# Two hybrid-mixer layers on one core: gates computed ahead by halves, one merge for all branches, another order in attention

## The chip, the cores and the metric

The kernel runs on one core of one Trainium2 chip. The metric is device time in microseconds of a whole execution, all weights and inputs in the chip's main memory at its start. Three executions of the kernel before were timed, and one more was profiled.

## The reference

Two layers of a hybrid mixer over 1024 latent tokens and 256 context tokens, model width 1024, in float32. In each layer the normalized and modulated input goes through one projection `w_in`, which feeds four branches of width 256: neighbourhood attention (A), latent attention (B), a bidirectional recurrent unit (C) and grouped-query attention (D). Each branch's result `y` is gated and merged:

```python
def merge_branches(ys, z, m, w_branch, w_out):
    zs = jnp.split(z, N_BRANCH, axis=-1)
    ms = jnp.split(m, N_BRANCH, axis=-1)
    acc = sum(jax.nn.sigmoid(ms[i]) * ((ys[i] * jax.nn.silu(zs[i])) @ w_branch[i]) for i in range(N_BRANCH))
    return acc @ w_out
# x <- LayerNorm(alpha * x + gate * merge_branches(...)) * ln_g + ln_b
```

The merge gates `m` are 4 x 1024 columns of the input projection, the largest part of it. In the first layer the context tokens take part in everything (1280 tokens, 10 tiles of 128); in the second the context has no output, so queries, gates and results are 1024 tokens (8 tiles). `shift`, `scale` and `gate` come from a small modulation product per layer.

## The kernel before, in words

Every float32 operand of a matmul is split in two parts, `hi` (ScalarE's cast to fp32r) and `lo` (VectorE's difference), and a product is three matmuls: hi x hi, hi x lo, lo x hi (`mm_a`, lines 276 to 278, tokens in rows; `mm_b`, lines 284 to 286, tokens in columns). `hi_lo` (lines 289, 290) splits activations, `split_w` (lines 238, 239) weights. The input of a layer is kept on the chip, split, as `xh` and `xl`.

A planner orders the instructions of each engine from the program text and gives tiles their buffers; a pool's tag has a fixed number of buffers, and an instruction that needs one waits until it is free. `wp` holds ten pairs of weight tiles (`whi`, `wlo`, 512 columns each) and two tiles for raw weights, `sl` 13 slots of 1280 columns for everything long (keys, values, probabilities, the sum, results), `tp` the short ones (`tmp` 3, `ph` 2, `pl` 2, `q` 3 buffers). `wide` is three banks of PSUM, taken in turn by `sbank`; `mm` has two more.

One layer runs: `g_proj` (projection of branch D), then `m_proj` and `a_proj` (B and A) woven with `lru` (C), then attention, then the merge, `last` and `outp`.

Attention works through twelve heads (four each of D, B, A), each in units of two or three query tiles; in the first layer a head begins with a short unit, the two context tiles with their 256 keys. For each query tile `scores` fills `wide` (line 639), VectorE copies it with the minimum (line 641), ScalarE takes the exponential (line 615). `values` then works through the blocks of 128 keys: `turn` transposes the probabilities (line 586) and splits them into `ph` and `pl`, `product` multiplies with the values (lines 593, 594). It is queued, and `pump` lets steps of it run between the scores of the following unit; each product follows its transposes by one block:

```python
            for i, b in enumerate(blocks):
                nx = turn(*b)
                tick()
                if st:
                    product(i - 1, *st)
                st = nx
                yield
```

`tick` draws from a generator that fills TensorE's time: `gates` computes the merge gates of the last two branches in `M_ORDER` = (2, 3, 1, 0), all eight chunks of 128 columns each, and stores them to memory (`gate_d`). `fetch` loads the next unit's queries and `ahead_kv` the next head's keys and values, both from SP's queue (lines 651, 653; 660, 665); the gates' weights are loaded, and the gates stored, from ScalarE's queue.

The merge goes through the first three branches, chunk by chunk and, within a chunk, by groups of tokens (256, 512 and 512 in the first layer, 512 and 512 in the second). For branches 2 and 3 a group is 24 matmuls for the gate (into `mm`) and 6 for the branch's product (into `wide`); for branch 1 the gate is loaded and 6 matmuls are left. ScalarE takes the sigmoid (line 993), VectorE multiplies (line 999), and the sum `acc[c]` is added to (line 1000), on POOL where the gate was loaded. In the first layer `modulation` steps are woven in. `last` does branch 0 in the same way with its own loop, and splits each chunk of the finished sum into `xh` and `xl` while it goes. `outp` multiplies with `w_out` tile by tile, two halves of 512 columns, adds the residual and normalizes (lines 1062 to 1071, statistics at line 197); for the first layer it also forms the next layer's `xh` and `xl`.

Of the kernel before, what the change touches and what calls it, by code (L numbers as in the profile page):

```python
# [16 lines left out]
D = 1024  # L17
# [19 lines left out]
G_PRE = 2  # L37
W_A = 30
W_B = 26
UNITS = [(2, 3), (5, 3), (8, 2)]  # L40
NBIAS = (E_N + M_N) * 64
# [5 lines left out]
def hybrid_kernel(ctx: ExitStack, tc, a):  # L47
# [8 lines left out]
    sm = ctx.enter_context(tc.tile_pool(name="sm", bufs=6))  # L56
# [60 lines left out]
    def spare():  # L117

        turns[0] += 1
        tag = ("tmp", "ph", "tmp", "pl", "tmp", "ph", "pl")[turns[0] % 7]  # L120
        return tp.tile([128, 512], F32, tag=tag, name=nm("spare"), bufs=3 if tag == "tmp" else 2)
# [72 lines left out]
    def row_stats(src):  # L194
        st = sm.tile([128, 2, 6], F32, tag="bnst", name=nm("bnst"))
# [36 lines left out]
    def split_w(raw, shape):  # L232
# [3 lines left out]
        hi = wp.tile([128, 512], F32R, tag="whi", name=nm("whi"))  # L236
        lo = wp.tile([128, 512], F32R, tag="wlo", name=nm("wlo"))
# [7 lines left out]
    def load_w(src, shape):  # L245
# [8 lines left out]
        return split_w(raw, shape)  # L254
# [37 lines left out]
    def layer(l, xh, xl, need_ctx, gate, finish, side, side2, ahead=None):  # L292
# [24 lines left out]
        gate_d = {i: dram([KC, 128, NT], F32, f"gates{i}") for i in M_ORDER[4 - G_PRE:]}  # L317
        u_d = [dram([2, 128, NT], F32, f"u{i}") for i in range(4)]

        def put_t(dst, t, first, src, rows=128):  # L320
# [6 lines left out]
            hi = tp.tile([128, 4, 128], F32R, tag="ph", name=nm("th"), bufs=2)  # L327
# [8 lines left out]
        def put_v(dst, t, src3):  # L336

            n = src3.shape[1]
            vt = tp.tile([128, 4, 128], F32R, tag="ph", name=nm("vt"), bufs=2)
# [226 lines left out]
        def attend(h, unit, qs, y, rcp, scores, vt):  # L566
# [7 lines left out]
            queue.append([values(64 * (h % 2), y, qts, blocks, pts, vt), len(blocks) + 1])  # L574

        def values(o, y, qts, blocks, pts, vt):
# [5 lines left out]
            def turn(vb, q0, cols):  # L582
# [4 lines left out]
                ph = tp.tile([128, 512], F32R, tag="ph", name=nm("ph"), bufs=2)  # L587
# [128 lines left out]
        def m_steps():  # L716
            gm, mrope_c, mrope_s, wraws, wu = pre[0]
            wm = [split_w(r, [128, 416]) for r in wraws]
# [23 lines left out]
            def second(t, has_q, y, kr):  # L742
# [4 lines left out]
                ch = tp.tile([128, 512], F32R, tag="ph", name=nm("ch"), bufs=2)  # L747
# [138 lines left out]
        def attention(jobs):  # L886
# [68 lines left out]
        for _ in att:  # L955
            pass
# [276 lines left out]
```

## Time and profile before

| | us |
|---|---|
| median of 3 runs | 3145.56 |
| lowest, highest | 3131.25, 3148.48 |
| profiled execution, its time | 3149.83 |
| its span, first to last instruction | 3148.0 |
| merge and `last`, first layer | 1157 to 1634 |
| attention, first and second layer | 423 to 1157, 2100 to 2738 |
| merge and `last`, second layer | 2738 to 3046 |

The mean granted clock of TensorE over the span is 0.949 of full speed. In what is cited from the trace, a name such as `m_att__ph` is a tile `ph` made in stage `m_att`, an arrow points from what is read to what is written (out<-in), L290 is line 290 of the kernel, and a bracket or a last column says how long the engine was idle and what ended that. PE is TensorE's matmuls, PEld its weight loads, DVE VectorE, ACT ScalarE, POOL GpSimd, SPq and ACTq the queues in which SP and ScalarE issue transfers. A busy time of PE is not full use: matmuls overlap, and one that stands with 0.39 us follows another every 0.23 us.

### The profile page before, as it was taken

The numbers are of one execution on the slowest core, as the hardware profiler recorded it, in microseconds if no ns is written. First come the engines' busy times: TensorE is split into PE (matmuls) and PEld (weight loads), VectorE is DVE, ScalarE is ACT, GpSimd is POOL, SyncE is SP. The second block draws the span as 40 slices with busy tenths as digits, with TensorE's granted clock in tenths as the row PEclk, the third lists the DMA queues.
The fourth block names the chain that finished last, engine by engine and source line by source line (L and its number), as shares of the span: only waits on it lengthen the run. The fifth ranks groups of instructions, "written<-read, shape, count | busy, mean of one in ns | idle before, by whom it ended". The sixth has DMA issues, their size and how long they took to land.

```text
span 3148.0 us, 39813 instructions
## 1 busy us (share of the span) xinstructions
PE 2837.8 (90%) x14458; PEld 2292.2 (73%) x14458; DVE 1554.1 (49%) x3147; ACT 1270.7 (40%) x2698; POOL 235.2 (7%) x327
## 2 busy tenths in 40 slices
PE   7987979998988999999789897998999897999878
PEld 3766868787877787776457685877887786788657
DVE  5653365554545551222368644366654464523366
ACT  4353364544444451111233435265544454512230
POOL 1210000000000000000342110000000000000141
PEclk9998989998999999999799999998999998999999
DMA  7232422222323222322462323322332233212252
GB/s 256 86 106 88 118 66 65 83 89 67 92 85 97 92 94 65 71 60 90 157 173 78 119 75 115 112 83 72 89 94 75 84 102 96 78 47 64 89 159 77
DMA packets 308782, 299.83 MB, mean 95 GB/s; under 512 B 24553, under 2 KB 245993, under 8 KB 308585
## 3 DMA queue, kind: packets, MB, share of 16 engines
q1 hardware_dynamic: 177384, 202.49, 21.3%
q10 hardware_dynamic: 131200, 94.79, 9.8%
q8 instruction: 114, 1.87, 0.3%
q14 instruction: 84, 0.68, 0.1%
HBM read 217.11 MB, written 80.10 MB: 94 GB/s over the span
## 4 chain that ended last, share of the span: by engine, by line
PE 65%; DMA 15%; DVE 7%; ACT 4%; POOL 3%; issue 3%; SPq 2%; ACTq 1%; POOLq 0%; DVEq 0%
PE wide L639 5%; PE merge__mm L284 4%; PE merge__mm L285 4%; PE merge__mm L286 4%; PE wide L284 2%; PE wide L285 2%; PE wide L286 2%; PE m_att__t L586 2%; PE a_att__mm L284 2%; PE a_att__mm L285 2%; PE a_att__mm L286 2%; DMA g_att__q<-start__qkg 2%; PE g_att__t L586 2%; PE m_att__mm L286 2%; PE m_att__mm L284 2%
## 5 line engine op out<-in xcount | busy, mean ns | idle before, releaser
L284 PE MATMUL merge__mm<-xh,merge__whi 128*128 128x512 f32 (+1 forms) x640 | 240.5, 376 | 1.2 <-DVE a_att__tmp L439 1.2
L285 PE MATMUL merge__mm<-xl,merge__whi 128*128 128x512 f32 (+1 forms) x640 | 236.7, 370 | 0.0
L286 PE MATMUL merge__mm<-xh,merge__wlo 128*128 128x512 f32 (+1 forms) x640 | 236.6, 370 | 0.0
L290 DVE TENSOR_TENSOR m_att__pl<-m_att__t,m_att__ph 128x384 fp32r<-128x384 f32 (+1 forms) x248 | 121.5, 507 | 141.3 <-ACT m_att__ph L289 138.2
L289 ACT CAST m_att__ph<-m_att__t 128x384 fp32r<-128x384 f32 (+1 forms) x248 | 105.7, 441 | 148.1 <-PE m_att__t L586 101.0
L238 ACT CAST merge__whi<-merge__wraw 128x512 fp32r<-128x512 f32 (+1 forms) x112 | 59.3, 530 | 236.0 <-PE merge__mm L285 179.3
L284 PEld LDWEIGHTS merge__mm<-xh,merge__whi 128*128 128x128 f32 x640 | 121.1, 189 | 41.5 <-issue 16.5
L239 DVE TENSOR_TENSOR merge__wlo<-merge__wraw,merge__whi 128x512 fp32r<-128x512 f32 (+1 forms) x112 | 64.5, 576 | 166.2 <-ACT merge__whi L238 158.4
L290 DVE TENSOR_TENSOR g_att__pl<-g_att__t,g_att__ph 128x384 fp32r<-128x384 f32 (+1 forms) x228 | 112.8, 514 | 68.0 <-ACT g_att__ph L289 64.6
L999 DVE TENSOR_TENSOR merge__tmp<-wide,merge__tmp 128x512 f32<-128x512 f32 (+1 forms) x80 | 50.9, 637 | 176.2 <-PE wide L286 168.3
L639 PE MATMUL wide<-g_att__ks,g_att__q 128*128 128x512 f32 (+1 forms) x400 | 112.4, 380 | 26.6 <-DMA g_att__q<-start__qkg 14.0
L286 PEld LDWEIGHTS merge__mm<-xh,merge__wlo 128*128 128x128 f32 x640 | 121.3, 189 | 20.7
L289 ACT CAST g_att__ph<-g_att__t 128x384 fp32r<-128x384 f32 (+1 forms) x228 | 99.6, 446 | 89.5 <-PE g_att__t L586 80.4
L285 PEld LDWEIGHTS merge__mm<-xl,merge__whi 128*128 128x128 f32 x640 | 121.2, 189 | 19.1
L284 PE MATMUL wide<-merge__uh,merge__whi 128*128 128x512 f32 (+1 forms) x240 | 100.5, 419 | 36.9 <-DVE merge__tmp L999 26.4
L284 PE MATMUL a_att__mm<-xh,a_att__whi 128*128 128x512 f32 (+1 forms) x320 | 126.2, 395 | 0.3 <-DVE a_att__tmp L439 0.3
L993 ACT ACTIVATE merge__tmp<-merge__mm 128x512 f32<-128x512 f32 (+1 forms) x80 | 44.2, 553 | 199.6 <-PE merge__mm L286 198.4
L593 PE MATMUL m_att__pv<-m_att__ph,m_att__vs 128*128 128x384 f32 (+1 forms) x228 | 88.8, 389 | 37.3 <-ACT m_att__ph L289 37.2
L285 PE MATMUL a_att__mm<-xl,a_att__whi 128*128 128x512 f32 (+1 forms) x320 | 121.9, 381 | 0.0
L641 DVE TENSOR_SCALAR_CACHE_REDUCE m_att__p<-wide 128x1280 f32<-128x1280 f32 (+1 forms) x72 | 98.7, 1371 | 46.1 <-PE wide L639 43.1
L286 PE MATMUL a_att__mm<-xh,a_att__wlo 128*128 128x512 f32 (+1 forms) x320 | 121.1, 380 | 0.0
L639 PE MATMUL wide<-m_att__ks,m_att__q 128*128 128x512 f32 (+1 forms) x400 | 120.8, 372 | 0.4 <-DVE m_att__p L641 0.4
(415 smaller groups left out, 8060.7 us busy)
## 6 DMA issues: line engine op xcount, KB each, us to landing
merge__wraw<-in_w_in_dram SPq DMA_DIRECT2D x64, 256.0 KB
mod__wm<-in_w_mod_dram SPq DMA_DIRECT2D x48, 256.0 KB
g_proj__wm<-in_w_mod_dram SPq DMA_DIRECT2D x16, 512.0 KB
a_att__wraw<-in_w_in_dram ACTq DMA_DIRECT2D x32, 256.0 KB
last__wraw<-in_w_out_dram SPq DMA_DIRECT2D x32, 256.0 KB
g_att__wraw<-in_w_in_dram ACTq DMA_DIRECT2D x28, 256.0 KB
m_att__wraw<-in_w_in_dram ACTq DMA_DIRECT2D x28, 256.0 KB
merge__wraw<-in_w_branch_dram SPq DMA_DIRECT2D x48, 128.0 KB
```

The costliest lines, as they stand in the source:

```text
L238: act.copy(hi[:, :n], raw[:, :n])
L239: dve.tensor_sub(lo[:, :n], raw[:, :n], hi[:, :n])
L284: pe.matmul(ps, wh, xh, start=first and k == 0, stop=False)
L285: pe.matmul(ps, wh, xl, start=False, stop=False)
L286: pe.matmul(ps, wl, xh, start=False, stop=last and k == nk - 1)
L289: act.copy(hi, src)
L290: dve.tensor_sub(lo, src, hi)
L586: pe.transpose(tb[:, i * 128:(i + 1) * 128], pts[q0 + i][:, col:col + 128], ident)
L593: pe.matmul(pv[:, qr], vt[:, vb, :], ph, start=i == 0, stop=False)
L639: pe.matmul(wide[:, c0:c0 + w], qs[:, j, qi * 128:(qi + 1) * 128], k[:, c0:c0 + w], start=j == 0, stop=j == len(ks) - 1)
L641: dve.tensor_scalar(pt[:, :nk], wide[:, :nk], -scale, None, ALU.mult, ALU.min, accum_out=nb)
L999: dve.tensor_mul(sgm[:, :g[1]], pb[:, :g[1]], sgm[:, :g[1]])
```

## The change

Gates computed ahead: `gate_d` has a tile for each odd chunk of every branch instead of all chunks of two branches, and `gates` goes through these. The merge goes through all four branches with computed (even) and loaded (odd) chunks in turn; `last` keeps only the loads of `w_out` and the splitting of the sum, by groups of 256 tokens over all eight chunks, after the whole merge. The second layer's modulation gate, which ran within `last`, is woven into the merge. `outp` begins with a batch of four tiles, first halves before second halves. In attention `product` follows `turn` by `AHEAD` = 2 blocks, `ph` has three buffers, `ahead_kv` is called at a head's second unit instead of its first, and TensorE's instructions keep the order of the program text (`manual_schedule`). `wp` has six pairs instead of ten, `sl` 16 slots instead of 13, and a `far` weight pair lies in a slot. Buffers of small tiles (`sm`, `bnst`) and the scratch of POOL's transfers shrink to make room.

```diff
-G_PRE = 2
+AHEAD = 2
...
-    wp = ctx.enter_context(tc.tile_pool(name="wp", bufs=10))
-    sl = ctx.enter_context(tc.tile_pool(name="sl", bufs=13))
+    wp = ctx.enter_context(tc.tile_pool(name="wp", bufs=6))
+    sl = ctx.enter_context(tc.tile_pool(name="sl", bufs=16))
...
-    def split_w(raw, shape):
+    def split_w(raw, shape, far=False):
...
-        hi = wp.tile([128, 512], F32R, tag="whi", name=nm("whi"))
-        lo = wp.tile([128, 512], F32R, tag="wlo", name=nm("wlo"))
+        if far:
+            both = slot(F32R, w=1024, s="wboth")
+            hi, lo = both[:, :512], both[:, 512:]
+        else:
+            hi = wp.tile([128, 512], F32R, tag="whi", name=nm("whi"))
+            lo = wp.tile([128, 512], F32R, tag="wlo", name=nm("wlo"))
...
-        return [load_w(w2[k * 128:(k + 1) * 128, c0:c0 + n], [128, n]) for k in range(KC)]
+        return [load_w(w2[k * 128:(k + 1) * 128, c0:c0 + n], [128, n], k >= 4) for k in range(KC)]
...
-        gate_d = {i: dram([KC, 128, NT], F32, f"gates{i}") for i in M_ORDER[4 - G_PRE:]}
+        gate_d = {(i, c): dram([128, NT], F32, f"gates{i}{c}") for i in M_ORDER for c in range(1, KC, 2)}
...
-            queue.append([values(64 * (h % 2), y, qts, blocks, pts, vt), len(blocks) + 1])
+            queue.append([values(64 * (h % 2), y, qts, blocks, pts, vt), len(blocks) + AHEAD])
...
-                ph = tp.tile([128, 512], F32R, tag="ph", name=nm("ph"), bufs=2)
+                ph = tp.tile([128, 512], F32R, tag="ph", name=nm("ph"), bufs=3)
...
-            st = None
+            turned = []
             for i, b in enumerate(blocks):
-                nx = turn(*b)
+                turned.append(turn(*b))
                 tick()
-                if st:
-                    product(i - 1, *st)
-                st = nx
+                if len(turned) > AHEAD:
+                    product(i - AHEAD, *turned.pop(0))
                 yield
-            product(nb - 1, *st)
+            for j, st in enumerate(turned):
+                product(nb - len(turned) + j, *st)
+                if j < len(turned) - 1:
+                    yield
...
                 if i == 0:
+                    head = begin(kv[label, h])
+                if i == 1:
                     j = jobs.index(job) + 1
                     if j < len(jobs):
                         ahead_kv(j)
-                    head = begin(kv[label, h])
...
-        for _ in att:
-            pass
-        flush()
+        with tc.manual_schedule(engines={mybir.EngineType.PE}):
+            for _ in att:
+                pass
+            flush()
...
-            for bi, i in enumerate(M_ORDER[:3]):
+            for bi, i in enumerate(M_ORDER):
                 uh, ul = load_u(i)
                 for c in range(KC):
-                    w = None if i in gate_d else load_chunk(w_in, C_GATE + i * D + c * 128)
+                    w = None if (i, c) in gate_d else load_chunk(w_in, C_GATE + i * D + c * 128)
...
-        weave((f"merge{l}", merge(), 72), (f"mod{l}", side, 50))
+        for _ in fill["gen"]:
+            pass
+        weave((f"merge{l}", merge(), 4 * KC * len(qgroups)), (f"mod{l}", side, 68))
...
-        (the loop of branch M_ORDER[3], with its splits, modulation steps and loads of w_out)
+        wo = [[load_w(a["w_out"][l, k * 128:(k + 1) * 128, h * 512:h * 512 + 512], [128, 512], h > 0 or 2 <= k < 6)
+               for k in range(KC)] for h in range(2)]
+        for g in qgroups:
+            for c0 in range(g[0], g[0] + g[1], 256):
+                for c in range(KC):
+                    hi_lo(xh[:, c, c0:c0 + 256], xl[:, c, c0:c0 + 256], acc[c][:, c0:c0 + 256])
...
+        batches = [range(q0t, q0t + 4)] + [range(t, t + 1) for t in range(q0t + 4, TT - 2)]
+        batches += [range(TT - 2, TT)] if need_ctx else [range(t, t + 1) for t in range(TT - 2, TT)]
+        for batch in batches:
+            pairs = [(t, slot(w=D, s="Y")) for t in batch]
             for h in range(2):
...
```

## Rows read from the trace of the kernel before

**Rows 1.** The page's busy times over the span.

```profile
PE 2837.8 (90%) x14458; PEld 2292.2 (73%) x14458; DVE 1554.1 (49%) x3147; ACT 1270.7 (40%) x2698; POOL 235.2 (7%) x327
```

**Rows 2.** Busy time by stretch, the merges: length; PE, PEld, DVE, ACT, POOL; clock.

```profile
1157.00:1325.00 168.00, 165.26 (x865) 130.94 (x863) 38.97 (x66) 33.35 (x65) 0.61 (x1) 1.00 0.29 76
1325.00:1485.00 160.00, 154.43 (x721) 117.05 (x721) 43.31 (x77) 26.48 (x53) 0.00 (x0) 0.97 0.24 61
1485.00:1634.00 149.00, 116.25 (x442) 68.97 (x441) 67.44 (x102) 52.98 (x103) 58.75 (x48) 0.81 0.60 175
2738.00:2955.00 217.00, 215.62 (x948) 177.91 (x949) 63.83 (x104) 46.87 (x87) 0.00 (x0) 1.00 0.21 57
2955.00:3046.00 91.00, 61.73 (x210) 40.23 (x209) 54.27 (x67) 38.05 (x65) 41.01 (x30) 0.91 0.51 157
```

**Rows 3.** Timeline of two loaded groups, second layer: start, duration, instruction, idle before.

```profile
2984.38 0.50 PE L284 MATMUL wide<-merge__uh,merge__whi 128*128 128x512 f32 x1 [0.87 <-DVE merge__tmp L999]
...
2986.14 0.69 DVE L999 TENSOR_TENSOR merge__tmp<-wide,merge__tmp 128x512 f32<-128x512 f32 x1 [1.81 <-PE wide L286]
...
2986.89 0.50 PE L284 MATMUL wide<-merge__uh,merge__whi 128*128 128x512 f32 x1 [0.85 <-DVE merge__tmp L999]
2986.91 1.29 POOL L1000 TENSOR_TENSOR merge__acc<-merge__acc,merge__tmp 128x512 f32<-128x512 f32 x1 [1.15 <-DVE merge__tmp L999]
```

**Rows 4.** Waits by pair, loaded stretches of both layers: total, times, longest.

```profile
ACT merge__tmp L993 <- DMA merge__tmp<-outp__gates: 24.3, 14, 3.4
ACT merge__tmp L993 <- DMA merge__tmp<-start__gates: 34.4, 19, 3.7
```

**Rows 5.** Busy time by stretch, the attention of both layers.

```profile
423.00:1157.00 734.00, 673.16 (x3857) 573.22 (x3857) 397.10 (x895) 366.05 (x818) 11.54 (x33) 0.95 0.27 84
2100.00:2738.00 638.00, 588.29 (x3182) 488.87 (x3180) 357.10 (x772) 328.39 (x712) 9.81 (x28) 0.96 0.28 86
```

**Rows 6.** Waits of TensorE in attention: four of layer 0, two of layer 1.

```profile
PE m_att__pv L593 <- ACT m_att__ph L289: 20.6, 3, 10.1
PE wide L639 <- DMA g_att__q<-start__qkg: 14.0, 4, 5.9
PE a_att__pv L593 <- ACT a_att__ph L289: 11.4, 2, 6.9
PE wide L639 <- DVE g_att__p L641: 9.8, 2, 8.6
...
PE m_att__pv L593 <- ACT m_att__ph L289: 16.6, 4, 5.9
PE a_att__pv L593 <- ACT a_att__ph L289: 15.8, 3, 6.4
```

**Rows 7.** Timeline of one such wait, layer 0.

```profile
719.54 2.19 SPq L665 DMA_DIRECT2D m_att__vs<-start__vm  x1
721.77 15.28 SPq L653 DMA_DIRECT2D m_att__q<-start__qkm  x1
...
745.28 0.37 ACT L289 CAST m_att__ph<-m_att__t 128x256 fp32r<-128x256 f32 x1 [10.09 <-DMA m_att__q<-start__qkm]
745.69 0.42 DVE L290 TENSOR_TENSOR m_att__pl<-m_att__t,m_att__ph 128x256 fp32r<-128x256 f32 x1 [10.04 <-ACT m_att__ph L289]
...
745.71 0.58 PE L593 MATMUL m_att__pv<-m_att__ph,m_att__vs 128*128 128x256 f32 x1 [9.16 <-ACT m_att__ph L289]
```

**Rows 8.** Groups by form, ScalarE, 1566 to 1650: busy, mean ns; idle before.

```profile
L289 ACT CAST xh<-merge__acc 128x256 fp32r<-128x256 f32 x8 | 3.1, 401 | 5.2 <-POOL merge__acc L1027 5.2
```

**Rows 9.** Groups by form, VectorE, output projection of the first layer.

```profile
L197 DVE BATCH_NORM_STATS2 outp__bnst<-outp__Y 128x6 f32<-128x512 f32 x40 | 26.5, 684 | 0.4
L1070 DVE SCALAR_TENSOR_TENSOR outp__Y<-outp__Y,outp__mv,outp__ln_g 128x512 f32<-128x512 f32 x20 | 14.4, 748 | 0.3
```

**Rows 10.** Groups by form, VectorE, attention of the first layer.

```profile
L641 DVE TENSOR_SCALAR_CACHE_REDUCE m_att__p<-wide 128x1280 f32<-128x1280 f32 x32 | 47.7, 1491 | 29.5 <-PE wide L639 28.4 <-PE m_att__t L586 0.8
```

**Rows 11.** Groups by form, ScalarE, attention of the first layer.

```profile
L615 ACT ACTIVATE m_att__p<-m_att__p,m_att__nb 128x1280 f32<-128x1280 f32 x32 | 43.8, 1367 | 20.5 <-DVE m_att__p L641 20.1
```

**Rows 12.** Waits of TensorE, projections of the first layer.

```profile
PE m_proj__t L326 <- DVE m_proj__tl L290: 11.9, 2, 10.0
```

More of the change, by code (lines that the diff above doesn't have):

```diff
@@ L120, in spare @@
         tag = ("tmp", "ph", "tmp", "pl", "tmp", "ph", "pl")[turns[0] % 7]
-        return tp.tile([128, 512], F32, tag=tag, name=nm("spare"), bufs=3 if tag == "tmp" else 2)
+        return tp.tile([128, 512], F32, tag=tag, name=nm("spare"), bufs=2 if tag == "pl" else 3)
     def bank():
@@ L194, in row_stats @@
     def row_stats(src):
-        st = sm.tile([128, 2, 6], F32, tag="bnst", name=nm("bnst"))
+        st = sm.tile([128, 2, 6], F32, tag="bnst", name=nm("bnst"), bufs=2)
         for i in range(2):
@@ L290, in hi_lo, with layer @@
         dve.tensor_sub(lo, src, hi)
-    def layer(l, xh, xl, need_ctx, gate, finish, side, side2, ahead=None):
+    def layer(l, xh, xl, need_ctx, gate, finish, side, ahead=None):
         w_in = a["w_in"][l]
@@ L338, in put_v @@
             n = src3.shape[1]
-            vt = tp.tile([128, 4, 128], F32R, tag="ph", name=nm("vt"), bufs=2)
+            vt = tp.tile([128, 4, 128], F32R, tag="ph", name=nm("vt"), bufs=3)
             hi_lo(vt[:, :n, :64], vt[:, :n, 64:], src3)
@@ L717, in m_steps @@
             gm, mrope_c, mrope_s, wraws, wu = pre[0]
-            wm = [split_w(r, [128, 416]) for r in wraws]
+            wm = [split_w(r, [128, 416], k >= 4) for k, r in enumerate(wraws)]
             def first(t, ps):
@@ L1045, in layer @@
                 bcast(ts[h], a[src][l, h * 512:(h + 1) * 512], 512)
-        gt, pairs = None, []
-        for t in range(q0t, TT):
-            if gt is None or t == CT:
-                gt = [tp.tile([128, 512], F32, tag="q", name=nm("gt"), bufs=3) for _ in range(2)]
-                for h in range(2):
-                    bcast(gt[h], gd[1 if t < CT else 0, h * 512:(h + 1) * 512], 512)
-            pairs.append((t, slot(w=D, s="Y")))
-            if need_ctx and t == TT - 2:
-                continue
+        gt = {}
+        batches = [range(q0t, q0t + 4)] + [range(t, t + 1) for t in range(q0t + 4, TT - 2)]
+        batches += [range(TT - 2, TT)] if need_ctx else [range(t, t + 1) for t in range(TT - 2, TT)]
+        for batch in batches:
+            pairs = [(t, slot(w=D, s="Y")) for t in batch]
             for h in range(2):
@@ L1057, in layer @@
                 for t, Y in pairs:
+                    s = 1 if t < CT else 0
+                    if s not in gt:
+                        gt[s] = tp.tile([128, 1024], F32, tag="q", name=nm("gt"), bufs=3)
+                        bcast(gt[s], gd[s], 1024)
                     ps = bank()
@@ L1072, in layer @@
                 finish(t, Y, later)
-            pairs = []
         while later:
@@ L1132, in later_mods @@
         yield from modulation(1, 0, 2048, mc1, raw_w, 512)
+        yield from modulation(1, 2048, 1024, gate1, raw_w, 512)
     def fin0(t, Y, later):
@@ L1143, in hybrid_kernel @@
     fin0.x_rows = rows0
-    layer(0, xh, xl, True, gate0, fin0, later_mods(), modulation(1, 2048, 1024, gate1, raw_w, 512), start())
+    layer(0, xh, xl, True, gate0, fin0, later_mods(), start())
     def fin1(t, Y, later):
@@ L1152, in hybrid_kernel @@
     fin1.x_rows = lambda t, hs: x1[(t - CT) * 128:(t - CT + 1) * 128, hs]
-    layer(1, xh, xl, False, gate1, fin1, iter(()), iter(()))
+    layer(1, xh, xl, False, gate1, fin1, iter(()))
 def _constants(np):
```

75 lines of the change are left out of this document (23 added, 52 removed).

## The prediction

> **What bounds the kernel now.** I read the page's head first. TensorE is busy for 90% of the span [rows 1]: the kernel is bound by TensorE, and what a change can win is the time in which TensorE has nothing to do or runs at the lower of its two levels, 1.2 instead of 2.4 GHz. The change adds and removes almost no matmuls: before, two branches had all eight gate chunks computed ahead, 2 x 8 = 16 chunks; now four branches have four each, again 16. So the question is only where TensorE waits.
>
> Second, the table of stretches [rows 2]. In the merge of layer 1, while gates are computed, TensorE hardly rests: 948 matmuls in 217 us, 0.229 us each, at clock 1.00. In layer 0, with the modulation woven in and groups of 256 columns among those of 512, 865 matmuls take 168 us, 0.194 us each. As soon as the branches with loaded gates come, that ends: 2955 to 3046 is 91 us for 210 matmuls (0.43 us each), and 1485 to 1634 is 149 us for 442 (0.34 us each), at clock 0.91 and 0.81.
>
> Third, the timeline of such a stretch [rows 3] shows why. A loaded group has six matmuls of its own, and the next group's first matmul waits 0.85 us for VectorE's multiply of the one before; POOL's add takes 1.29 us beside it. The two groups shown start 2.5 us apart, and TensorE works for 1.65 of these. ScalarE waits for the gates to land 24.3 us in this stretch and 34.4 us in that of layer 0 [rows 4]. Nothing else is there for TensorE to do: the other branches' gates are finished.
>
> Fourth, attention, the longest part: 734 us and 638 us at clock 0.95 and 0.96 [rows 5]. What TensorE waits for there [rows 6]: the queries' loads, 14.0 us, and the scores behind them 9.8; ScalarE's casts of the turned probabilities (ph), 20.6 + 11.4 us in layer 0 and 16.6 + 15.8 us in layer 1. The queue of SP [rows 7] shows what is behind it: keys and values of the next head are issued ahead of pieces of the next queries, which then sit in the queue for 15.28 us, and ScalarE stands idle for 10.09 us until that traffic lets it go on, with TensorE idle 9.16 us behind it.
>
> **The change part by part.**
>
> Merge. Now every odd chunk's gates are loaded and every even chunk's computed, in all four branches, so a loaded chunk of 18 (layer 0) or 12 (layer 1) matmuls always stands between two computed ones of 90 or 60, and the separate last branch is gone. If TensorE then keeps the pace of its full stretches all the way: layer 0 has 865 + 721 + 442 = 2028 matmuls in 477 us from 1157 to 1634 [rows 2], at 0.194 us that is 393 us, 84 less. Layer 1 has 948 + 210 = 1158 in 308 us, at 0.229 us 265 us, 43 less. Together 127 us. Two things are to be taken off. (a) The sum can be split for the output projection only when all branches are done: one multiply 0.69, one POOL add 1.29, eight casts of 256 columns at 0.40 us and a last difference of 0.42 [rows 3, 7, 8], 5.6 us a layer in which TensorE has nothing, 11 us in all. The splits behind the first 256 columns (32 or 24 more casts) hide behind the 24 matmuls of each half tile, 24 x 0.229 = 5.5 us; without that cover they would cost 0.40 each, 22 us over both layers. (b) The 0.85 us wait between loaded products stays as a dependency. There are 48 + 32 = 80 such groups; uncovered that is 68 us, covered by the next computed chunk's gate matmuls nothing. I take a quarter, 17 us, because the two banks for computed gates are free just then. 127 - 11 - 17 = 99 us gained; between 37 (b in full and the splits uncovered) and 116 (b nothing).
>
> The loads of the later branches' u find four free slots of 16 (eight for the sum, four for the u in use) where 13 left one; what that wins is not counted apart, since it is inside the pace taken.
>
> Output projection. First four tiles by their first half, then by their second, instead of single tiles: the same matmuls, and the second half's weights load behind 4 x 5.5 us of first halves. But the normalization of the first four tiles starts only after the fourth, and VectorE's part of it is four statistics of 0.68 and four operations of 0.75 us a tile in layer 0 [rows 9], 5.7 us, 23 us for four, which then stand beside the splits' differences. TensorE's own 11 us a tile leave VectorE little to catch up with. I take 10 us lost, between 0 and 23.
>
> Attention. Keys and values of the next head are asked for one unit later. In layer 0 the first unit of a head is the two short context tiles, so the queries of the long unit that follows no longer sit behind the keys and values. That is aimed at the 14.0 + 9.8 us of the queries. The ScalarE waits have the same traffic as their cause, and that traffic is not less, it comes a unit later. Products follow their transposes by two turns instead of one, with three buffers for ph (two for pl as before), and TensorE runs in the order of the program text instead of the planner's. One turn more of slack is three transposes and two products; what it must cover is a cast of 0.37 and a difference of 0.42 us for 256 columns [rows 7], or, when an exponential of 1.37 us and a reduction of 1.49 us come first [rows 10, 11], some 3.7 us. I take 25 us gained: the queries' 24 us and nothing net from order and depth. The bounds are wide: all waits of rows 6 gone is 56 + 32 = 88 us; on the other side, each of the 128 long scores (32 + 32 a layer [rows 10], two layers alike) holding TensorE for one exponential is 128 x 1.37 = 175 us lost.
>
> Smaller pools. Weight pairs drop from ten to six, with half of each projection's weights in slots of the pool that also serves the recurrent branch and the latent projection. There TensorE already waits up to 10.0 us at a time for tiles that leave by DMA [rows 12]. I take 8 us lost, between 0 and 40 (one such wait more in each of two stages of two layers).
>
> **Sum.** The profiled execution took 3149.83 us, 4 above the median of the runs shown, 3145.56. 3149.8 - 99 + 10 - 25 + 8 = 3044; I forecast 3040, on the side of that median.
>
> One rule speaks against the attention part. Rows 7 show SP's queue and ScalarE's held up by the same loads. The Trainium skill (DMA: Bandwidth & Descriptors, section Issuing engines are not separate DMA queues) says that transfers issued from different engines run on the same 16 DMA engines and interleave, and that issuing from several saves only issue time; the trace agrees, since ScalarE's 10.09 us ended with a load that SP had issued. By that rule alone the attention term would be 0 instead of 25, which is rival 1.
>
> **The rivals.**
> 1. The stalls only move: keys and values are as large as before and meet the gates' weights and stores one unit later. For it: most of the waits in rows 6 are of ScalarE, not of queries; against it: a long unit gives the queries more time. 3149.8 - 99 + 10 + 8 = 3069. Chance 0.2.
> 2. The stalls go altogether, covered by the further turn and the later keys: 3149.8 - 99 + 10 - 88 + 8 = 2981, and some 20 lower if the clock then stays up (0.05 of 734 us and 0.04 of 638 us are lost to it now, 62 us in all, most of it with the waits [rows 5]). Chance 0.15.
> 3. Loaded products stay uncovered (b in full): 3044 + 51 = 3095. For it: these products wait for the multiply just before although their buffer has three banks [rows 3]; against it: the planner has other matmuls to put there. Chance 0.12.
> 4. The pools are too small in the projections: 3044 + 32 = 3076. For it the wait of rows 12; against it the slots that grew from 13 to 16. Chance 0.08.
> 5. The other side: in attention TensorE, now in written order, waits at each long score for the exponential that ScalarE has ahead of its casts. Place: the first product after each score; price up to 1.37 us, 175 us in all. The rest gains 99 - 10 - 8 = 81 us, so from 0.63 us a score on the kernel is not faster; in full, 3149.8 - 81 + 175 = 3244. For it: VectorE and ScalarE are each busy for half of the attention [rows 5], so they seldom answer at once; against it: two turns lie between. Chance 0.1. The Trainium skill (TensorE: Matmul & The Clock Gate, section Step-by-step: what each phase is for) says that matmuls stay in program order and only weight loads are pulled ahead, by which a blocked product holds all that is written behind it, this rival's mechanism.
>
> **How the numbers follow.** The forecast itself has 0.35; cases 1, 3 and 4 lie within 55 us above it, case 2 some 60 to 80 below. Half of case 5 (a part of its price) ends within 0.5%, 16 us, about what a measurement of this kernel can tell from no change; most of the rest above. So faster 0.84, within 0.5% 0.06, slower 0.10. The range leaves out 0.1 at each end: below it reaches to 2955, into case 2 with part of the clock; above to 3135, case 3 with a pool stall in.
>
> **What would show it.** Right: the merge's stretches at clock 1.00 and near 0.19 and 0.23 us a matmul; POOL's adds spread over the merge; no queries of a long unit 15 us in SP's queue; one TensorE gap of 5 to 8 us at each merge's end. Wrong: TensorE waiting for ph or pl many times by a microsecond in attention; 0.85 us at every loaded group; new gaps before weight casts in the projections; VectorE full in the output projection with TensorE waiting for Y. The largest single risk is the written order in attention, whose cost no row of before shows.

## The result

| | median us | lowest to highest | ratio to before, 95% interval |
|---|---|---|---|
| before, beside the changed kernel | 3140.98 | 3131.25 to 3148.48 | |
| changed | 3270.67 | 3266.66 to 3274.97 | 1.0415 [1.0379, 1.0451] |

The change made the kernel 4% slower. The forecast was 3040 with a range from 2955 to 3135. The profiled execution's span went from 3148.0 to 3266.2 us, 118 more, at almost the same mean clock (0.949, now 0.955). The lines of the changed kernel that are cited most lie five to eight further down: the split of activations is L294 and L295 (was L289, L290), a score L646 and L648 (L639, L641), the exponential L622 (L615), the transposes L591 (L586), the products L598 and L599.

The page's busy times, changed kernel (before: [rows 1]):

```profile
PE 2849.3 (87%) x14458; PEld 2284.0 (70%) x14458; DVE 1571.1 (48%) x3207; ACT 1274.2 (39%) x2738; POOL 206.8 (6%) x307
```

The same matmuls, and to about 1% the same work on the three main engines: what was added is mostly waiting. Cut into stages at each stage's first TensorE matmul, and for attention at its first transposes (its first scores start 8 to 20 us before), the spans give (lengths worked out from the trace; the windows shown below differ from the stages by up to 2 us):

```
us                            before   changed   difference   forecast
projections, both layers     428+350   464+377      +63          +8
attention, both layers       735+643   797+704     +123         -25
merge and output projection  583+409   545+379      -68         -89
sum                                                +118        -106
```

Busy time by stretch of the changed kernel: projections, attention, merge, each of layer 0 and then 1; length; PE, PEld, DVE, ACT, POOL; clock, DMA share, GB/s:

```profile
0.00:464.00 464.00, 361.94 (x1746) 276.62 (x1746) 208.23 (x458) 179.76 (x374) 39.45 (x79) 0.88 0.36 114
464.00:1261.00 797.00, 699.50 (x3929) 582.95 (x3929) 401.88 (x894) 361.86 (x810) 11.89 (x34) 0.97 0.24 76
1261.00:1660.00 399.00, 387.04 (x1928) 291.51 (x1927) 143.33 (x256) 109.28 (x228) 40.35 (x33) 0.99 0.41 117
...
1806.00:2181.00 375.00, 307.94 (x1528) 253.05 (x1528) 176.38 (x363) 155.08 (x344) 31.77 (x56) 0.89 0.31 92
2181.00:2887.00 706.00, 604.06 (x3225) 491.55 (x3224) 359.03 (x765) 324.23 (x703) 9.58 (x28) 0.98 0.25 77
2887.00:3155.00 268.00, 264.92 (x1132) 209.54 (x1133) 110.83 (x182) 84.36 (x159) 32.10 (x22) 1.00 0.32 96
```

The merges are what was forecast: clock 0.99 and 1.00, TensorE busy 387 of 399 and 265 of 268 us (before, the loaded stretches had 0.81 and 0.91 [rows 2]). Attention is longer than in [rows 5] though its clock rose to 0.97 and 0.98, so the loss there is not the clock. TensorE's idle time in it (length less busy time) grew from 61 to 98 us and from 50 to 102 us; its busy time grew too, by 26 and 16 us for about the same matmuls, and that part was not looked into. In the projections of layer 0 TensorE works about as much as before, but in 36 us more, and at clock 0.88 (before 0.95).

What TensorE waited for in attention, changed kernel, layer 1 (total, times, longest):

```profile
PE m_att__t L591 <- DVE m_att__pl L295: 35.9, 22, 8.1
PE g_att__t L591 <- DVE g_att__pl L295: 19.9, 19, 2.3
PE a_att__t L591 <- DVE a_att__pl L295: 16.4, 21, 1.8
```

These three are 72 us in 62 waits. Before, in the same layer, the pair stands once:

```profile
PE g_att__t L586 <- DVE g_att__pl L290: 4.9, 1, 4.9
```

There the waits were few and long [rows 6]. Now they are many, for the transposes of a later block: these need a bank that a former block's split has not yet emptied. In layer 0 of the changed kernel the same three pairs are only 29 us, in 38 waits; there the scores' waits for the reduction of the score before are larger, 36 us in 16 waits. One of the waits for a bank in the timeline (start, duration, instruction, idle before and its releaser), changed kernel, layer 1, behind a long score:

```profile
2441.18 1.49 DVE L648 TENSOR_SCALAR_CACHE_REDUCE m_att__p<-wide 128x1280 f32<-128x1280 f32 x1 [1.01 <-PE wide L646]
...
2442.86 1.36 ACT L622 ACTIVATE m_att__p<-m_att__p,m_att__nb 128x1280 f32<-128x1280 f32 x1
...
2443.05 0.49 PE L591 MATMUL m_att__t<-ident,m_att__p 128*128 128x128 f32 x3
...
2444.68 0.48 ACT L294 CAST m_att__ph<-m_att__t 128x384 fp32r<-128x384 f32 x1
...
2445.19 1.07 DVE L295 TENSOR_TENSOR m_att__pl<-m_att__t,m_att__ph 128x384 fp32r<-128x384 f32 x2 [1.51 <-ACT m_att__ph L294]
...
2445.81 0.55 PE L591 MATMUL m_att__t<-ident,m_att__p 128*128 128x128 f32 x3 [1.92 <-DVE m_att__pl L295]
2446.11 0.48 PE L289 MATMUL m_att__mm<-xh,m_att__whi 128*128 128x512 f32 x1
```

VectorE reduces the score, ScalarE takes the exponential of 1.36 us, and the cast that has to empty the transposes' bank comes only at 2444.68, the difference after it. TensorE stands for 1.92 us in front of the next transposes. Right behind them in the text are six gate matmuls, the first at 2446.11, that need nothing of all this. A planned order can put them into the gap; the written one can't. The Trainium skill (TensorE: Matmul & The Clock Gate, section Step-by-step: what each phase is for) says that matmuls stay in program order; the rows agree, since all six run only behind the wait of 1.92 us.

In the projections, what TensorE waits for longest before attention, waits by pair, changed kernel, layer 0:

```profile
PE a_proj__mm L281 <- ACT a_proj__wboth L243: 17.8, 2, 17.0
```

The timeline that leads to the longer of these two waits, same kernel (ACTq is the issue of a transfer from ScalarE's queue):

```profile
272.65 11.11 ACTq L338 DMA_DIRECT2D start__qkm<-m_proj__tl  x2
283.12 0.28 DVE L295 TENSOR_TENSOR m_proj__tl<-m_proj__t,m_proj__th 32x128 fp32r<-32x128 f32 x1 [10.50 <-DMA start__qkm<-m_proj__tl]
283.79 1.28 ACT L530 ACT_TABLE_LOAD   x1 [10.44 <-DVE m_proj__tl L295]
285.09 1.36 ACT L530 ACTIVATE lru__lrug<-lru__lrug,lru__ca 128x1280 f32<-128x1280 f32 x1
286.36 1.12 ACT L243 CAST a_proj__wboth<-a_proj__wraw 128x512 fp32r<-128x512 f32 x2
...
287.01 0.80 PE L281 MATMUL a_proj__mm<-a_proj__wboth,xh 128*128 128x512 f32 x1 [16.97 <-ACT a_proj__wboth L243]
```

`wboth` is a `far` weight pair in a slot. Its cast stands on ScalarE behind two stores, a table load and an exponential (of branch C). The stores take 11.11 us to issue, since the second is of a difference that VectorE can only form at 283.12, when an earlier store has given back a buffer of `tl`. Layer 1 has a wait of the same pair with 12.5 us. Only a part of the 17.0 us is due to the far pair: before, TensorE waited 10.0 us at this place, for `tl` itself [rows 12], and with the pools of before, in e3 below, another tile waits there behind the same stores:

```profile
273.39 0.47 PE L331 MATMUL a_proj__t<-ident,a_proj__tmp 128*128 128x128 f32 x1 [10.08 <-ACT a_proj__tmp L819]
```

### The profile page after: what moved, and what is told of

The parts are those of the page before. It is cut to its first block, busy times and chain, and to the rows that moved or that the text cites. A ratio compares the mean times of both kernels' runs of the same rounds, so it can differ in the third digit from the quotient of the medians.

```text
span 3266.2 us, 40198 instructions
## 1 busy us (share of the span) xinstructions
PE 2849.3 (87%) x14458; PEld 2284.0 (70%) x14458; DVE 1571.1 (48%) x3207; ACT 1274.2 (39%) x2738; POOL 206.8 (6%) x307
## 5 line engine op out<-in xcount | busy, mean ns | idle before, releaser
L289 PE MATMUL merge__mm<-xh,merge__whi 128*128 128x512 f32 (+1 forms) x640 | 240.2, 375 | 1.0 <-ACT a_att__tmp L945 1.0
L290 PE MATMUL merge__mm<-xl,merge__whi 128*128 128x512 f32 (+1 forms) x640 | 236.6, 370 | 0.0
L295 DVE TENSOR_TENSOR m_att__pl<-m_att__t,m_att__ph 128x384 fp32r<-128x384 f32 (+1 forms) x248 | 123.3, 508 | 163.3 <-ACT m_att__ph L294 76.0
L295 DVE TENSOR_TENSOR g_att__pl<-g_att__t,g_att__ph 128x384 fp32r<-128x384 f32 (+1 forms) x228 | 114.9, 516 | 127.8 <-ACT g_att__ph L294 59.3
L243 ACT CAST merge__whi<-merge__wraw 128x256 fp32r<-128x256 f32 (+1 forms) x128 | 65.8, 514 | 250.7 <-PE merge__mm L290 173.3
L294 ACT CAST m_att__ph<-m_att__t 128x384 fp32r<-128x384 f32 (+1 forms) x248 | 105.8, 440 | 138.7 <-PE m_att__t L591 123.7
L1007 DVE TENSOR_TENSOR merge__tmp<-wide,merge__tmp 128x512 f32<-128x512 f32 (+1 forms) x120 | 76.4, 637 | 172.7 <-PE wide L291 158.2
L289 PEld LDWEIGHTS merge__mm<-xh,merge__whi 128*128 128x128 f32 x640 | 120.7, 189 | 42.0 <-issue 17.8
L591 PE MATMUL m_att__t<-ident,m_att__p 128*128 128x128 f32 x616 | 108.4, 284 | 45.7 <-DVE m_att__pl L295 39.4
L289 PE MATMUL wide<-merge__uh,merge__whi 128*128 128x256 f32 (+1 forms) x320 | 126.7, 396 | 17.4 <-ACT merge__uh L294 12.0
L294 ACT CAST g_att__ph<-g_att__t 128x384 fp32r<-128x384 f32 (+1 forms) x228 | 98.1, 446 | 107.2 <-PE g_att__t L591 104.6
L244 DVE TENSOR_TENSOR merge__wlo<-merge__wraw,merge__whi 128x256 fp32r<-128x256 f32 (+1 forms) x128 | 72.0, 563 | 139.2 <-ACT merge__whi L243 133.3
L290 PEld LDWEIGHTS merge__mm<-xl,merge__whi 128*128 128x128 f32 x640 | 120.9, 189 | 20.1
L591 PE MATMUL g_att__t<-ident,g_att__p 128*128 128x128 f32 x616 | 106.7, 282 | 31.6 <-DVE g_att__pl L295 29.5
L289 PE MATMUL a_att__mm<-xh,a_att__whi 128*128 128x512 f32 (+1 forms) x320 | 126.2, 394 | 6.7 <-DVE a_att__tmp L444 6.7
L646 PE MATMUL wide<-g_att__ks,g_att__q 128*128 128x512 f32 (+1 forms) x400 | 98.4, 383 | 37.4 <-DVE g_att__p L648 32.4
L648 DVE TENSOR_SCALAR_CACHE_REDUCE m_att__p<-wide 128x1280 f32<-128x1280 f32 (+1 forms) x72 | 98.7, 1371 | 66.4 <-PE wide L646 66.4
L646 PE MATMUL wide<-m_att__ks,m_att__q 128*128 128x512 f32 (+1 forms) x400 | 112.4, 363 | 20.6 <-DVE m_att__p L648 19.9
L295 DVE TENSOR_TENSOR a_att__pl<-a_att__t,a_att__ph 128x384 fp32r<-128x384 f32 (+2 forms) x204 | 93.0, 463 | 77.6 <-PE a_att__pv L599 45.2
L591 PEld LDWEIGHTS m_att__t<-ident,m_att__p 128*128 128x128 f32 x616 | 73.9, 143 | 71.6 <-DVE m_att__pl L295 59.8
```

The costliest lines, as they stand in the source:

```text
L243: act.copy(hi[:, :n], raw[:, :n])
L244: dve.tensor_sub(lo[:, :n], raw[:, :n], hi[:, :n])
L289: pe.matmul(ps, wh, xh, start=first and k == 0, stop=False)
L290: pe.matmul(ps, wh, xl, start=False, stop=False)
L294: act.copy(hi, src)
L295: dve.tensor_sub(lo, src, hi)
```

## The experiments

Theory W: the written order of attention costs most of the loss, the pools the rest. Rival D: depth 2 with two `pl` buffers makes the waits, whatever the order.

**e1, the planner's order.** The one wrapper is removed, all else is as changed.

```diff
-        with tc.manual_schedule(engines={mybir.EngineType.PE}):
-            for _ in att:
-                pass
-            flush()
+        for _ in att:
+            pass
+        flush()
```

> The changed kernel with one thing undone: in attention TensorE's order is the planner's again. The changed kernel took 3270.7 us, 130 more than before; by its trace attention took 113 us more (797 and 706 us against 735 and 658), the projections with the start of attention 96 more, the merge with the output projection 94 less. Theory W (written order): TensorE waits at its transposes for VectorE's differences because it has to keep the text's order; with the planner's order attention falls back to about 735 and 655 us, the whole to about 3155. Rival D (depth): two blocks between transposes and products with only two pl buffers is what holds the transposes, whatever the order; then at most 20 us come back, 3250.

3080.36 us, ratio 0.982 [0.9784, 0.9857]: 190 us less than the changed kernel and faster than before. The attention stretches of this run:

```profile
463.00:1169.00 706.00, 672.11 (x3888) 572.58 (x3887) 397.58 (x894) 359.77 (x810) 11.82 (x34) 0.96 0.27 86
2094.00:2704.00 610.00, 576.94 (x3203) 482.53 (x3201) 358.41 (x773) 322.94 (x707) 9.56 (x28) 0.97 0.29 90
```

797 became 706 and 704 became 610 us: the order alone costs 185 us by stages, more than theory W had taken (whose 655 us for layer 1 comes from another cut than the 643 above), and the waits for `pl` in layer 1 fall from 72 to 4.6 us:

```profile
PE g_att__t L591 <- DVE g_att__pl L295: 4.2, 1, 4.2
PE a_att__t L591 <- DVE a_att__pl L295: 0.2, 1, 0.2
PE m_att__t L591 <- DVE m_att__pl L295: 0.2, 1, 0.2
```

Of the 185 us, some 133 are TensorE's idle time (98 and 102 us of it in the changed kernel, 34 and 33 in e1). Rival D as it was put, whatever the order, falls, since depth and buffers are unchanged here. But the two `pl` buffers have a part of their own in the written order. The text puts the product that gives a `pl` buffer back behind the transposes whose split needs that buffer, and VectorE waits for it; changed kernel, layer 1:

```profile
DVE m_att__pl L295 <- PE m_att__pv L599: 26.3, 17, 2.5
DVE a_att__pl L295 <- PE a_att__pv L599: 25.2, 20, 2.1
DVE g_att__pl L295 <- PE g_att__pv L599: 20.2, 12, 2.0
```

These are 72 us of VectorE in 49 waits; in e1 the same pairs are 6 us in 9 waits, and before there are none. A third `pl` buffer was not tried in the written order, so how much of the 185 us hangs on it is not known.

**e2, one block of lag, in the written order.**

```diff
-AHEAD = 2
+AHEAD = 1
```

> The changed kernel with products one block behind their transposes instead of two (AHEAD = 1), written order kept. Theory W: the written order is the cause and the shorter distance gives it less slack: no gain, 3270 or up to 40 more. Rival D: with one block of distance a pl buffer is free before it is wanted, the waits of transposes for VectorE's difference (72 us of row totals in layer 1) go, and the whole falls by 60 to 110 us, to 3160 to 3210.

3308.32 us, ratio 1.055 [1.0509, 1.0591], 38 us slower than the changed kernel. The waits of TensorE in layer 1's attention go over to the products:

```profile
PE m_att__pv L598 <- ACT m_att__ph L294: 33.7, 26, 7.4
PE a_att__pv L598 <- ACT a_att__ph L294: 21.2, 25, 2.1
```

So the further block eases the written order by 38 us; it isn't what makes it slower than the planner's.

**e3, the pools of before, in the written order.** The same without `far` pairs in the projections, and in the first half of `w_out`.

```diff
-    wp = ctx.enter_context(tc.tile_pool(name="wp", bufs=6))
-    sl = ctx.enter_context(tc.tile_pool(name="sl", bufs=16))
+    wp = ctx.enter_context(tc.tile_pool(name="wp", bufs=10))
+    sl = ctx.enter_context(tc.tile_pool(name="sl", bufs=13))
...
-        return [load_w(w2[k * 128:(k + 1) * 128, c0:c0 + n], [128, n], k >= 4) for k in range(KC)]
+        return [load_w(w2[k * 128:(k + 1) * 128, c0:c0 + n], [128, n]) for k in range(KC)]
```

> The changed kernel with the pools of before: ten weight pairs, 13 slots, all projection weights in the weight pool, the second half of w_out in slots; attention and merge as changed. Theory P (pools): the 17.0 and 12.5 us gaps before weight casts of the neighbourhood projection and the late first scores (12.8 us) come from slots, so the projections and the start of attention fall back by about 90 us, the whole to about 3180; the merge may lose some 10 us at the loads of u. Rival Q: they come from the written order that begins at attention's first instruction and from what stands before it; then less than 30 us come back, 3240 or more.

3226.25 us, ratio 1.0283 [1.0246, 1.0321]: 44 us back, between the two expectations. Layer 0's projections end at 428 us again instead of 464, and layer 1's take 361 instead of 377; attention is 5 and 10 us longer than in the changed kernel. So in the written order the pools cost the projections 36 + 16 = 52 us, not the 71 that e5's expectation below takes from this run.

**e4, the merge alone.** The kernel before with only the parts of gates, merge, `last` and `outp`; attention (planner's order, `AHEAD` 1, keys at the first unit, two `ph` buffers) and pools as before.

> The kernel before with the merge part alone: odd chunks of all four branches computed ahead, computed and loaded chunks in turn, no last branch apart, the sum split by groups, first four output tiles by halves; attention, pools and depth as before (13 slots, ten weight pairs, planner's order). If the merge's gain is its own: 94 us less than before, about 3050 (ratio 0.970). If it rested on the 16 slots, for the loads of u and for w_out: 50 us less or fewer, 3090 or more (ratio 0.983).

3066.82 us, ratio 0.9773 [0.9736, 0.981], 71 us less than its runs of before. The merges:

```profile
1161.00:1560.00 399.00, 386.23 (x1927) 290.62 (x1926) 140.43 (x252) 106.81 (x223) 39.23 (x33) 0.99 0.40 115
2687.00:2957.00 270.00, 266.45 (x1139) 211.03 (x1140) 113.22 (x188) 87.39 (x168) 32.09 (x22) 1.00 0.32 95
```

The same lengths as in the changed kernel to 2 us, so the merge's gain doesn't rest on the 16 slots or on attention's changes.

**e5, planner's order and the pools of before.** The edits of e1 and e3 together.

> The changed kernel with two parts taken back together: TensorE in the planner's order in attention (190 us in the run with only that) and the pools of the kernel before (71 us of projections, seen in the run with only the pools back). Merge, output projection, depth 2, three ph buffers and keys at the second unit stay. Theory A (the two costs are separate places and add): 3270.7 - 190 - 71 = 3010, 2995 to 3030, which is faster than every kernel so far (the least was 3066.8 with the merge alone and 3080.4 with the planner's order alone). Rival B (depth 2 and later keys win in attention only where the projections in front were late, so that with the pools back attention takes the 734 and 638 us of before): about 3065, as with the merge alone.

3049.73 us, ratio 0.9704 [0.969, 0.9719], the best of the versions up to here, but not 3010. The attention stretches:

```profile
423.00:1141.00 718.00, 670.90 (x3888) 570.94 (x3887) 398.07 (x900) 359.71 (x812) 12.08 (x34) 0.96 0.27 86
2040.00:2672.00 632.00, 584.42 (x3204) 488.28 (x3204) 360.86 (x778) 325.52 (x711) 9.72 (x28) 0.96 0.28 88
```

Against e1 the projections win 40 + 23 us (463 to 423, 376 to 353), and attention loses 12 + 22 us (706 to 718, 610 to 632). The pools are a trade: the projections are shorter with ten pairs and 13 slots, attention with six pairs and 16 slots. That attention wins by the slots, in which it holds keys, values and probabilities, is likely but was not tried apart from the weight pairs. That the two costs simply add (theory A) is wrong; rival B, attention as before, is nearer, since 718 and 632 are only 28 us below 735 and 643.

**e6 and e7, what the keys' time and the depth bring.** Each is e5 with one part undone.

```diff
-                if i == 0:
-                    head = begin(kv[label, h])
-                if i == 1:
+                if i == 0:
                     j = jobs.index(job) + 1
                     if j < len(jobs):
                         ahead_kv(j)
+                    head = begin(kv[label, h])
```

> As the run with the planner's order and the old pools, but the next head's keys and values asked for at a head's first unit, as before. If the later keys bring what the attention wins in the planner's order (28 + 28 us by stages): 40 to 60 us slower than that run, with the queries in SP's queue for 15 us again. If the depth of two brings it: within 10 us of it.

3050.47 us, ratio 0.9704 [0.969, 0.9719], the same as e5 to the last digit of the ratio: in the planner's order the later keys bring nothing over the whole. By the profiles of one execution each they win 11 us of attention in layer 0 (718 against 729) and lose 10 in layer 1 (632 against 622).

```diff
-AHEAD = 2
+AHEAD = 1
```

> As the run with the planner's order and the old pools, but products one block behind their transposes instead of two (three ph buffers stay). If depth brings the gain of attention: 40 to 60 us slower. If the keys' time brings it: within 10 us, since the planner places the product where its cast is ready anyway. In the text's order the second block was worth 38 us.

3056.46 us, ratio 0.9726 [0.971, 0.9742]: 7 us, and the intervals overlap. In the planner's order the second block is worth about 7 us if anything, in the written order 38. That the keys' time changes little is seen in SP's queue. A piece of a long unit's queries in layer 0 of the changed kernel, with the later keys, stands behind keys and values again:

```profile
793.96 0.48 SPq L667 DMA_DIRECT2D m_att__ks<-start__qkm  x1
794.54 0.42 SPq L672 DMA_DIRECT2D m_att__vs<-start__vm  x1
795.01 15.27 SPq L660 DMA_DIRECT2D m_att__q<-start__qkm  x1
```

And one in e6, with the earlier keys:

```profile
712.89 15.04 SPq L660 DMA_DIRECT2D m_att__q<-start__qkm  x1
```

Both sit as long as the 15.28 us of [rows 7].

**e8 and e9, the exponential's cost doubled in either order.** After the exponential of each of the 128 long dense scores ScalarE copies the probabilities onto themselves; the values stay. e8 has the written order, e9 the planner's, both with the changed pools.

```diff
                 act.activation(pt[:, c0:c1], pt[:, c0:c1], AF.Exp, bias=nb, scale=scale, accum_out=total)
+                if c1 == NT:
+                    act.copy(pt[:, :NT], pt[:, :NT])
```

> The changed kernel, written order kept, with ScalarE's cost behind each of the 128 long dense scores doubled: the probabilities are copied onto themselves after the exponential, about 1.3 us more of ScalarE each, 165 us in all; the values are the same. Theory W2 (in the text's order TensorE stands at the transposes behind a score because the cast that frees their bank is queued behind the exponential): nearly the whole of it shows, 3270.7 + 80 to 165 = 3350 to 3435. Rival V (the wait is VectorE's: the 1.49 us reduction and the differences): ScalarE, busy for 362 of 797 and 324 of 706 us, takes it into its idle time, less than 40 us more. The same copy in the planner's order comes next as the control: there ScalarE's idle time should take it in, under 50 us.

> The control of the run with the doubled ScalarE cost behind each long score: the same copy, but TensorE in the planner's order (pools as changed), beside the 3080.4 us of the run with the planner's order alone. In the text's order the copy cost 63 to 68 us of its 165. If it is the order that exposes ScalarE (theory W2): under 30 us here, at most 3110. If ScalarE's load costs the same in either order: 60 to 70 us, about 3145, and the order's 190 us has little to do with the exponential.

e8: 3337.78 us, ratio 1.0617 [1.0599, 1.0634], 0.0202 above the changed kernel's ratio, some 63 us. e9: 3080.06 us, ratio 0.9838 [0.981, 0.9866]; e1 without the copy had 3080.36 and 0.982. The copy by form in e8 (one of the four groups of 32):

```profile
L624 ACT COPY m_att__p<-m_att__p 128x1280 f32<-128x1280 f32 x32 | 40.4, 1263 | 0.4
```

The attention stretches of e8, both layers:

```profile
465.00:1285.00 820.00, 703.10 (x3906) 582.53 (x3906) 398.76 (x889) 432.99 (x870) 11.94 (x34) 0.97 0.23 74
2213.00:2959.00 746.00, 625.42 (x3220) 507.09 (x3218) 357.61 (x761) 391.79 (x764) 9.58 (x28) 0.95 0.23 72
```

Those of e9:

```profile
463.00:1169.00 706.00, 669.23 (x3892) 571.44 (x3892) 396.41 (x894) 431.71 (x873) 11.86 (x34) 0.97 0.27 86
2094.00:2702.00 608.00, 573.67 (x3196) 480.29 (x3195) 352.63 (x767) 389.92 (x768) 9.58 (x28) 0.97 0.29 91
```

The copies are 128 x 1.26 = 162 us of ScalarE. In the written order attention grows by 23 + 40 us; in the planner's order ScalarE carries the same load (432 and 390 us busy in both) and attention stays at 706 and 608 us. So the order exposes ScalarE's work behind a score, as theory W2 says. But it exposes 63 of 162 us, 0.39, less than W2's 80 and more than rival V's 40: part of the wait belongs to something else. What the reduction on VectorE costs (rival V) was not doubled in the same way.

**e10, the output projection in single tiles.** e5 with

```diff
-        batches = [range(q0t, q0t + 4)] + [range(t, t + 1) for t in range(q0t + 4, TT - 2)]
+        batches = [range(t, t + 1) for t in range(q0t, TT - 2)]
```

> As the run with the planner's order and the old pools (3049.7 us), with the output projection begun in single tiles as before instead of four tiles by halves. If the batch costs what the stages show (146 and 108 us with it, 135 and 110 before): 5 to 15 us faster in the first layer, 3035 to 3045 in all. Rival: the second half's weights then come late, because the loads now begin only with the merge's end, and TensorE waits for them: the same or up to 20 us slower.

3041.53 us, ratio 0.9713 [0.9677, 0.975] against e5's 0.9704: no difference that the runs can tell; by stages the output projection takes 142 and 104 us, 4 less in each layer than in e5. The longest of TensorE's waits in the output projection of layer 0, in e5:

```profile
PE wide L281 <- DVE outp__Y L1049: 15.0, 5, 12.1
```

In e10:

```profile
PE outp__mm L281 <- ACT last__wboth L243: 6.9, 4, 3.9
PE wide L281 <- DVE outp__Y L1049: 3.5, 5, 1.2
```

The long wait for `Y` behind four tiles' normalization goes, and waits for the second half's weights come in its place: the rival of this run, in part.

## Why the prediction was wrong

**The failed step** is the attention term, in the words "nothing net from order and depth". The term was -25 us and came out as +123. Its parts by the runs: the written order +185 by stages (e1), the rest of the attention's changes with 16 slots -62 (e1 against before: 735 to 706, 643 to 610). Rival 5, given 0.1, had named the written order, with a price of 0 to 175 us; the order cost 185 to 190. Two things were missed.

First, the price was bounded by the exponentials of the long scores alone. e8 shows that the written order exposes 0.39 of what is added on ScalarE there; if the work that stands there already is exposed by the same share, of 128 x 1.37 us and the 128 x 0.19 us of accumulator reads behind them that would be about 78 us, an estimate from e8. The rest stands elsewhere and wasn't taken apart by a run: 47 of the 185 us lie in `a_att`, whose scores are shorter (243 against 221, 207 against 182 us), VectorE waits for the `pl` buffers (e1), and there are single long waits of scores for the reduction of the one before, this one in layer 0 of the changed kernel:

```profile
PE wide L646 <- DVE m_att__p L648: 19.8, 6, 13.4
```

Second, the argument against rival 5, that two turns lie between, looked at the products. The wait stands at the transposes. They take two banks in turn, so those of a block need the bank of the block two before, whose split must be done; between lies one turn, not two. With a lag of two the product of that former block stands right behind these transposes and needs the same split, so the transposes meet the wait first, and a larger lag can't help them.

**The queries' 24 us**, the gain in that term. TensorE's waits for the queries' loads did go, 14.0 us before [rows 6] and 0.6 in layer 0 of the changed kernel, but that is no gain in time: e6 puts the keys' time at nothing over the whole, and the 15 us loads are still there. Here rival 1 (the stalls only move) held. The rule of the Trainium skill cited there (DMA: Bandwidth & Descriptors, section Issuing engines are not separate DMA queues) gave the better value, 0. It speaks of issuing from several engines, though, and e6 shows only that the time of issue doesn't matter. That attention in the planner's order is still 28 us shorter than before (e5) is neither the keys (e6) nor much the depth (e7); what of it is the third `ph` buffer was not tried.

**The smaller pools**, taken at 8 with bounds of 0 and 40, cost 63 us in the projections: 36 and 27 by stages, and 40 and 23 between e1 and e5. The kind of loss was rival 4's, and one place was named (new gaps before weight casts: 17.0 and 12.5 us). The waits for these casts are 33 us in both layers (17.8 and 15.2), within the bound of 40, and a part of them stood there before for `tl`. Outside the bound lay what it left out: the first scores' wait for VectorE's reduction (14.8 us in layer 0 against 2.1 before), and the clock, 0.88 and 0.89 instead of 0.95 and 0.93. Unforeseen was the other side: the pools of the change give 34 us back in attention, so that their net is a loss of 31 us (3080.36 against 3049.73).

**The merge** was right in kind. It was forecast at 393 + 265 us plus 28 for (a) and (b), 686 in all, and took 399 + 270 = 669 up to the output projection's first matmul; its own last matmuls start 9 us later in each layer, among those of the output projection. Both deductions were too large. (a), the split of the sum, left no gap, because the first tiles' products ran among the last of the merge, as the changed kernel's timeline shows:

```profile
1661.19 0.40 PE L282 MATMUL outp__mm<-last__wlo,xh 128*128 128x512 f32 x1
...
1661.43 0.28 PE L289 MATMUL wide<-merge__uh,merge__whi 128*128 128x256 f32 x1
```

(b), the waits between loaded products, is 3.0 us in layer 0 and 2.3 in layer 1, and the longest wait of the merge is one for a branch's result; changed kernel, layer 0 from the merge's start to the end of the output projection:

```profile
PE wide L281 <- DVE outp__Y L1050: 17.7, 6, 14.9
PE wide L289 <- ACT merge__uh L294: 8.9, 3, 7.7
PE wide L289 <- DVE merge__tmp L1007: 3.0, 4, 1.5
```

That the gain of merge and output projection is still only 68 to 71 us, not 89, is because the 477 and 308 us of before ran to the end of `last`, while the output projection had begun at 1611 and 3038: 23 + 8 = 31 us of overlap, counted as if they were all to win. Cut where the output projection begins, the merge of before took 448 + 299 = 747 us. **The output projection** lost 11 us in layer 0 (135 to 146) and nothing in layer 1, where 10 in all was taken. The wait of 14.9 us for `Y` is the one forecast, but without the batch only 4 us a layer come back (e10), so what the other 7 in layer 0 are is open.

The sum with the measured terms: 3148.0 - 68 + 123 + 63 = 3266, the span that was found.

The chances didn't fit the prediction's own working either. Half of rival 5's 0.1 was to end within 0.5%, which leaves at most 0.05 and not 0.10 for slower; and with 0.16 for all that is not faster, the range could not leave out only 0.1 above 3135.

## What to carry to other kernels

Before TensorE's order is fixed by hand, count what stands written behind each matmul that can wait, and look for independent work that a planner now moves into such gaps: here 185 us hung on it, with the same matmuls and within 2% the same busy time of VectorE and ScalarE in attention. Ask for each buffer, the transposes' PSUM banks too, who empties it and what that engine has ahead of it, not only whether the next consumer has slack. When memory moves from one pool to another, price both stages; and when a stage is timed for its gain, end it where the next stage's first matmul starts.

## What the runs showed that was not expected

Added work on an engine that is busy for half of the time can be free or not by another engine's order alone: 162 us of copies on ScalarE cost nothing that the runs can tell (e9) or 63 us (e8). A store that waits on ScalarE's queue for its data also holds ScalarE's own instructions: 11.1 us at the store, 10.44 us idle before the next instruction of ScalarE, and 16.97 us on TensorE, for a weight cast that has nothing to do with that store. And with two `pl` buffers and two blocks of lag VectorE waited 72 us in layer 1 for products that the text puts behind the next transposes (changed kernel), 6 us with the planner's order (e1), and not at all with one block of lag (before and e2).
